# A two-layer encoder trunk: attention's DMAs in a written order, layer 0's 1/rms by TensorE, folds and transposes in the last chunk, norm weights in the splits

## The chip, the cores and the metric

The kernel runs on one core of a Trainium2 chip. Its engines are TensorE (matrix products, PE in the profile), VectorE (DVE), ScalarE (ACT), GpSimd (POOL) and SyncE (SP), which in this kernel issues nearly all DMA transfers. The metric is the device time of one execution in microseconds (us); lower is better.

## The reference

The input x has 2048 tokens of 1024 float32 values. Two layers are applied, then a final RMS norm:

```python
def rms_norm(x, g):
    y = x * lax.rsqrt(jnp.mean(x * x, axis=-1, keepdims=True) + EPS)
    return y * g

# layer 0: h = rms_norm(x, norm_even)
proj = h @ w_in                                   # 1024 -> 3072
a_x, a_b, a_c, a_z, b_u, b_z = jnp.split(proj, 6 parts of 512, axis=-1)
y_a = a_b * centred_depthwise_conv(a_c * a_x, conv_w) * silu(a_z)
f = jnp.fft.fft2(u, axes=(1, 3), norm="ortho").real     # u: b_u as (1, 2048, 4, 128)
y_b = f * silu(b_z)
x = x + jnp.concatenate([y_a, y_b], axis=-1) @ w_out

# layer 1: h = rms_norm(x, norm_odd)
q, k, v, z = jnp.split(h @ w_in, [1024, 1280, 1536], axis=-1)   # 8 q heads, 2 kv heads of 128
q = apply_rope(rms_norm(q, q_gain)); k = apply_rope(rms_norm(k, k_gain))
p = softmax(q k^T * 128 ** -0.5)                  # over all 2048 keys
x = x + ((p @ v) * silu(z)) @ w_out

return rms_norm(x, final_norm)
```

The product is computed to about float32 accuracy.

## The kernel before

**Layout and precision.** Activations are kept transposed: 128 features on the partitions, tokens along the free axis, in four token blocks of 512. Each float32 operand of a product is split into a high and a low part (`split`, lines 42 and 44: ScalarE casts the high part, VectorE or GpSimd subtracts for the low one), and each product is three matmuls (`mm3`, lines 58 to 60: high x high, high x low, low x high) into one PSUM bank. Large products take two token blocks and two halves of features and columns at once and need seven block multiplies in place of eight (class `Pairs`). The operands of the seven are named in the order in which they are multiplied: 11, s2, 12, s3, s1, 22, s4; their weights 11, t2, 21, t3, t1, t4, 22. A multiply of this kind has 24 matmuls of 512 columns. Raw weights are fetched four blocks of 512 KB at a time into a ring (`raw_weights`, line 266, with the DMA at 272) and then split (`split_weights`). A "hook" is a function run ahead of a named multiply.

**What sets the order.** TensorE's instructions run in program order through the whole kernel (`tc.manual_schedule` for PE). In stretches marked with a further `manual_schedule`, other engines do too: VectorE, ScalarE and GpSimd through the start of layer 0, VectorE and ScalarE through attention. Everywhere else a planner orders each engine's queue, SyncE's DMA issues among them, by its own cost estimates. Each engine then works its queue in that order.

**Layer 0's input projection** (`layer0_in`, to about 525 us). The first columns of u are multiplied for token blocks 0 and 1 while VectorE and ScalarE form the sums of squares in `accs`. `rstd_d` (lines 96 to 102) transposes a block's sums by TensorE, adds them, takes the power -0.5 on GpSimd and stores the result to DRAM; `bcast_d` (line 109) fetches it back, spread over all partitions. VectorE then applies norm and weight (line 427) and the operands are split. Chunks of `Pairs` products follow: the first pair of token blocks through chunks 0 to 3 and one for b_z, then the same for the second pair, 11 in all. For token blocks 2 and 3 the sums' mean and the broadcast are done by TensorE (`rstd_pe`, lines 113 to 139: eight one-column matmuls, a power, eight VectorE operations that form the identity scaled by 1/rms in two parts, and two matmuls with ones), in chunk 2's hooks ("s2" mean of 2, "s3" broadcast of 2, "s1" mean of 3, "12" broadcast of 3), and the operands of the second pair are prepared and stored in the hooks after that (`operands`, line 222). In chunk 0 the operand s1 is added in place over the raw 21, and s3 and s1 both are made ahead of the first multiply.

**The Fourier part** (525 to about 600 us). `fold` combines tokens and their mirror images of u, once per channel group; group 0's result is transposed by TensorE (line 770, into four PSUM banks), split, and multiplied by cosine and sine matrices. The folds of groups 0 and 1 stand in the program after layer 0's last chunk and are placed by the planner; the transposes of group 0 come after that chunk in TensorE's order.

**Layer 1's projection** (`layer1_in`, to about 1220 us). `raw_weights` scales each raw block in place by norm_odd on ScalarE (line 275, four passes per block), right behind the block's load; the split follows. q and k go through their norms and rotary positions (lines 1028 to 1065).

**Attention** (`Attention`, lines 1217 to 1386). There are 32 groups (16 query tiles of 128 x 2 kv heads), each with 4 heads x 4 blocks of 512 keys. The order of PE, VectorE and ScalarE is a list of steps per slot, four slots a group:

```python
SLOT = "O0 L2 E-3 G2 L3 T4 T5 S0 E-2 S1 M0 H4 E-1 S2 M1 O1 L4 S3 M2 F T6 H5 C0 T7 M3 O2 H6 N0 H7 O3 L5 E0".split()
DRAIN = "O0 L2 E-3 G2 L3 T4 T5 H4 H5 E-2 L4 O1 L5 F T6 T7 O2 E-1 H6 L6 O3 H7 W L7 W W".split()
```

S is a score product into one of four PSUM banks; M, C, N find the rows' maximum; E is the exponential on ScalarE into `praw` (line 1319), and every second E stores praw to the tile P by DMA (line 1322; the room in P comes free when T has read it). T transposes P (line 1330); H and L split it (ScalarE, VectorE); O multiplies by v. G (once per group) adds the row sums, stores their inverses `l` to DRAM (line 1370), fetches them back over all partitions as `lb` (1372), and fetches the gate z (1375). F is `finish` of the last group: ScalarE copies the output from PSUM over lb (1382), GpSimd multiplies it by the gate, and it is stored. T, H, L, O and G trail S by 26 key tiles. The next group's queries are loaded when its first S is reached. FIRST is the list of the first five slots; "X" there runs filler steps: products of z that were left for this place, counted by `nfill`. DRAIN is the list after the last group. SyncE's order is the planner's.

**The output projection and the end.** `layer1_out_start` (line 1388) fetches the first operands and weights; it stands behind the last full slot, and the W steps of DRAIN split them. `layer1_out` (line 1412) multiplies the first pair of token blocks, then the last blocks column by column (line 1498). `finish(tb)` (line 1432) applies the final norm to a finished block and stores it.

Of the kernel before, what the change touches and what calls it, by code (L numbers as in the profile page):

```python
# [15 lines left out]
F32 = mybir.dt.float32  # L16
F32R = mybir.dt.float32r
# [95 lines left out]
def rstd_pe(c, parts, tag, n):  # L113
# [11 lines left out]
    nc.gpsimd.tensor_tensor(r[:, 0:nj], m[:, 0:nj], c.mhalf[:, 0:nj], op=ALU.pow)  # L125
    rb = [c.small.tile([P, TB], F32R, tag="rb", name=f"rb_{tag}{i}") for i in "hl"]
# [15 lines left out]
WSKIP = 1  # L142
# [4 lines left out]
class Pairs:  # L147
# [118 lines left out]
    def raw_weights(self, src, raw_tiles=None, g=None):  # L266

        raw = {}
        for b in ("11", "21", "12", "22"):
# [3 lines left out]
            if g is not None:  # L273
                for i in range(4):
                    self.nc.scalar.activation(raw[b][:, i], raw[b][:, i], AF.Copy, scale=g[:, 4 * k + i:4 * k + i + 1])  # L275
        return raw

    def split_weights(self, W, op, t, name, lo_eng="dve"):
        W[op] = self.rooms.pop() if self.rooms else tuple(self.c.wp.tile([P, 4, TB // 2], F32R, tag="w", name=f"{name}_{op}{n}") for n in "hl")
        split(self.nc, t, W[op][0][:], W[op][1][:], lo_eng=lo_eng)  # L280

    def weight_ops(self, src, name, raw_tiles=None, lo_engs={}, g=None):


        raw = self.raw_weights(src, raw_tiles, g)
# [18 lines left out]
    def queue_weights(self, src, name, g):  # L304
# [3 lines left out]
        def start():  # L308
            raw.update(self.raw_weights(src, None, g))

        def step(b):
            return lambda: self.split_weights(W, b, raw[b], name)
# [7 lines left out]
    def all_weights(self, src, name, lo_engs={}, g=None):  # L320
        W, steps = self.weight_ops(src, name, lo_engs=lo_engs, g=g)
# [94 lines left out]
def layer0_in(c):  # L416
# [59 lines left out]

    def bcast(tb):
# [27 lines left out]
    bcast(0)  # L505
    ps = batch(c, wu, hrow(G[1]), "pu_1", {1: lambda: bcast(1)})
# [17 lines left out]
    W1 = []  # L524
    s2 = pair(), pair()
    d2 = lambda k: s2[k // 2][:, k % 2]

# [5 lines left out]

    def make1():
        for k in range(4):
            tt(nc.gpsimd, a21(k), a21(k), a22(k), add)
# [8 lines left out]
    def w1(*ops):  # L545
# [26 lines left out]

    bc = {}
# [1149 lines left out]
```

## Time and profile before

| | |
|---|---|
| three runs, us | 2387.48, 2389.18, 2394.09 (median 2389.18) |
| profiled execution, us | 2389.2, of which the span 2387.4 |
| TensorE busy | 2284.1 us, 96% of the span |
| VectorE | 1502.5 us, 63% |
| ScalarE | 1238.4 us, 52% |
| GpSimd | 562.1 us, 24% |

The span is the time from the first to the last instruction that the profile records. In rows of single instructions, the first number is the start in us from the span's start and the second the duration; then come engine, line of the kernel, operation, output<-inputs and shape. In rows of waits, "A <- B: total, times, longest" says that engine and instruction A stood until B had ended. SPq is SyncE's queue issuing DMAs. Rows of a stretch "from:to" list its length, the busy time and count of PE, PEld (weight loads), VectorE, ScalarE and GpSimd, and then TensorE's granted clock (1.00 is full speed), the mean busy share of the DMA engines and the GB/s moved.

### The profile page before, as it was taken

Reading aid. Unit: us, or ns where it says so; the run is one execution under the profiler, and the core shown is the slowest. Engines: PE = TensorE matmul, PEld = TensorE weight load, DVE = VectorE, ACT = ScalarE, POOL = GpSimd, SP = SyncE. Lnnn points to the kernel's source line nnn. Section 1 sums busy time; section 2 is a strip of 40 time slices with the busy share of each in tenths; the row PEclk is TensorE's granted clock in tenths of the full one; section 3 lists DMA queues with packets and bytes.
Section 4 is the critical chain, followed back from the end, with each engine's and each line's share of the span. In section 5 each row is a group of like instructions: output and inputs, shape, how many; then the busy total and the mean of one; then the engine's idle time right before and its main releaser. Section 6 shows DMA issues by size and latency. Waiting matters only on the chain. (4 is left out here: it accounts for less than half of the span.)

```text
span 2387.4 us, 34207 instructions
## 1 busy us (share of the span) xinstructions
PE 2284.1 (96%) x12438; PEld 1922.5 (81%) x12438; DVE 1502.5 (63%) x2335; ACT 1238.4 (52%) x2676; POOL 562.1 (24%) x418
## 2 busy tenths in 40 slices
PE   8889899998999989999999999999999999997998
PEld 6767788877888889889977878778788888886887
DVE  6867757679543335334437877777777777776235
ACT  5432433224333355445546777777777777775222
POOL 2455524444222122203201110000000001003212
PEclk9999999999999999999999999999999999999999
DMA  5245742166655443434465777777777777769553
GB/s 165 71 143 169 236 148 71 63 220 241 246 190 181 116 133 117 160 115 133 160 245 150 201 202 192 195 187 197 196 201 190 186 194 186 186 177 298 162 192 133
DMA packets 260568, 414.51 MB, mean 174 GB/s; under 512 B 37168, under 2 KB 157104, under 8 KB 258608
## 3 DMA queue, kind: packets, MB, share of 16 engines
q1 hardware_dynamic: 258128, 404.70, 57.3%
q0 software_dynamic: 1008, 6.55, 0.8%
q8 instruction: 99, 1.62, 0.3%
q10 hardware_dynamic: 1264, 1.07, 0.1%
q14 instruction: 69, 0.57, 0.1%
HBM read 191.45 MB, written 86.59 MB: 116 GB/s over the span
## 5 line engine op out<-in xcount | busy, mean ns | idle before, releaser
L1300 DVE TENSOR_REDUCE mx<-s 128x1 f32<-128x512 f32 x512 | 351.5, 687 | 186.9 <-PE s L60 182.7
L1319 ACT ACTIVATE praw<-s,nb,qs 128x512 f32<-128x512 f32 x512 | 400.3, 795 | 70.3 <-DMA P<-praw 52.4
L1342 ACT CAST pr<-t 128x512 fp32r<-128x512 f32 x512 | 288.2, 596 | 159.3 <-PE t L1330 159.2
L1346 DVE TENSOR_TENSOR pr<-t,pr 128x512 fp32r<-128x512 f32 x512 | 329.6, 680 | 31.4 <-ACT pr L1342 30.9
L58 PE MATMUL s<-kv,aq 128*128 128x512 f32 x512 | 215.3, 421 | 26.2 <-ACT praw L1319 22.5
L1330 PEld LDWEIGHTS t<-ident_r,P 128*128 128x128 f32 x2048 | 202.6, 140 | 40.3 <-DMA P<-praw 3.3
L58 PE MATMUL o<-pr,kv 128*128 128x512 f32 x512 | 212.9, 416 | 1.8 <-ACT pr L1342 1.7
L1330 PE MATMUL t<-ident_r,P 128*128 128x128 f32 x2048 | 204.4, 243 | 4.1 <-DMA P<-praw 3.1
L59 PE MATMUL o<-pr,kv 128*128 128x512 f32 x512 | 203.1, 397 | 0.2 <-DVE pr L1346 0.2
L60 PE MATMUL o<-pr,kv 128*128 128x512 f32 x512 | 203.2, 397 | 0.0
L60 PE MATMUL s<-kv,aq 128*128 128x512 f32 x512 | 203.2, 397 | 0.0
L59 PE MATMUL s<-kv,aq 128*128 128x512 f32 x512 | 202.1, 395 | 0.0
L275 ACT ACTIVATE ring_r<-ring_r,g1s 128x256 f32<-128x256 f32 x160 | 68.9, 498 | 188.8 <-DMA ring_r<-w 188.6
L1383 POOL TENSOR_TENSOR az<-az,lb 128x512 f32<-128x512 f32 x32 | 41.5, 1296 | 480.4 <-ACT lb L1382 480.4
L58 PEld LDWEIGHTS s<-kv,aq 128*128 128x128 f32 x512 | 96.3, 188 | 57.1 <-ACT praw L1319 37.4
L952 POOL TENSOR_TENSOR acc<-acc,sq 128x512 f32<-128x512 f32 x48 | 69.2, 1442 | 244.4 <-ACT sq L950 226.3
L60 PEld LDWEIGHTS o<-pr,kv 128*128 128x128 f32 x512 | 96.7, 189 | 23.4
L60 PEld LDWEIGHTS s<-kv,aq 128*128 128x128 f32 x512 | 96.8, 189 | 22.7
L58 PEld LDWEIGHTS o<-pr,kv 128*128 128x128 f32 x512 | 96.4, 188 | 19.2 <-ACT pr L1342 2.2
L59 PEld LDWEIGHTS o<-pr,kv 128*128 128x128 f32 x512 | 96.9, 189 | 17.8 <-DVE pr L1346 0.5
L1377 POOL TENSOR_TENSOR az<-az,lb 128x512 f32<-128x512 f32 x32 | 42.0, 1312 | 291.9 <-DMA lb<-ld 224.0
L1319 ACT ACTIVATION_READ_ACCUMULATOR praw<-s,nb,qs 128x1 f32 x512 | 110.5, 216 | 0.0
(639 smaller groups left out, 5869.6 us busy)
## 6 DMA issues: line engine op xcount, KB each, us to landing
P<-praw SPq DMA_DIRECT2D x256, 512.0 KB
ring_r<-w SPq DMA_DIRECT2D x80, 512.0 KB
ring_o<-x_T SPq DMA_DIRECT2D x32, 512.0 KB
ring_r<-wo SPq DMA_DIRECT2D x32, 512.0 KB
qT<-ring_o SPq DMA_DIRECT2D x64, 256.0 KB
aq<-qT SPq DMA_DIRECT2D x31, 512.0 KB
x1T<-po_t SPq DMA_DIRECT2D x16, 512.0 KB
a_x<-x1T SPq DMA_DIRECT2D x16, 512.0 KB
```

The lines of the kernel that those rows point to most:

```text
L58: nc.tensor.matmul(ps, lh, rh, start=first, stop=False, skip_group_check=shared)
L59: nc.tensor.matmul(ps, lh, rl, start=False, stop=False, skip_group_check=shared)
L60: nc.tensor.matmul(ps, ll, rh, start=False, stop=last, skip_group_check=shared)
L275: self.nc.scalar.activation(raw[b][:, i], raw[b][:, i], AF.Copy, scale=g[:, 4 * k + i:4 * k + i + 1])
L952: nc.gpsimd.tensor_tensor(a, a, sq, op=ALU.add)
L1300: self.nc.vector.tensor_reduce(st.mx[h][:, b:b + 1], st.banks[h, b][:], op=ALU.max, axis=AX.X)
L1319: self.exp = nc.scalar.activation(raw[:, b % 2], st.banks.pop((h, b))[:], AF.Exp, bias=st.nb[h][:], scale=self.c.qs[:, st.g[0], st.g[1], h ...
L1330: self.nc.tensor.transpose(pt[:, h * P:(h + 1) * P].bitcast(F32R), st.Ps[h // 2][:, h % 2, kt // 8, (kt % 8) * P:(kt % 8 + 1) * P], self.c ...
L1342: self.nc.scalar.copy(pr[:, 0], pt[:])
L1346: self.nc.vector.tensor_tensor(pr[:, 1], pt[:], pr[:, 0], op=ALU.subtract)
L1377: nc.gpsimd.tensor_tensor(st.zt[:], st.zt[:], st.rb[:], op=ALU.mult)
L1383: nc.gpsimd.tensor_tensor(st.zt[:], st.zt[:], st.rb[:], op=ALU.mult)
```

## The change

Layer 0: token blocks 0 and 1 get their mean and broadcast by `rstd_pe` too, as steps inside the second u batch; the inverse rms is stored to DRAM as well, for the later folds. The operand s1 has two tiles of its own, made on GpSimd ahead of chunk 0; the next chunk's weights are fetched from hook 1 on, and its weights t2, t3 are made one hook apart. In chunk 2, the broadcasts of blocks 2 and 3 stand two multiplies behind the means, and the four preparations of operands each come one hook or more later. The last chunk (number 10) gets hooks that run the folds of groups 0 and 1 and group 0's transposes, which become a function. The norm weights of layer 1 go from `raw_weights` to `split_weights`. One tile (rb_n1_1_2) is taken from another pool.

Attention: SLOT and DRAIN get the steps A (load the next group's queries), D (store the row sums' inverse), B (fetch them back, and z) and V (output stores that `finish` has queued); SyncE runs in program order through the loop. `layer1_out_start` moves three slots on, and its W steps start behind it. Seven filler steps in place of five run ahead of the first slot. The final norm of block 1 moves behind the second column of block 2.

```diff
-def rstd_pe(c, parts, tag, n):
+def rstd_pe(c, parts, tag, n, d=None):
...
     nc.gpsimd.tensor_tensor(r[:, 0:nj], m[:, 0:nj], c.mhalf[:, 0:nj], op=ALU.pow)
+    if d is not None:
+        nc.sync.dma_start(d[0:nj].rearrange("j t -> t j"), r[:, 0:nj])
...
-WSKIP = 1
...
-    def raw_weights(self, src, raw_tiles=None, g=None):
+    def raw_weights(self, src, raw_tiles=None):
...
-            if g is not None:
-                for i in range(4):
-                    self.nc.scalar.activation(raw[b][:, i], raw[b][:, i], AF.Copy, scale=g[:, 4 * k + i:4 * k + i + 1])
...
+    def split_weights(self, W, op, t, name, lo_eng="dve", g=None):
...
+        for i in range(4):
+            k = 4 * (int(op[0]) - 1) + i
+            self.nc.scalar.activation(hi[:, i], t[:, i], AF.Copy, scale=g[:, k:k + 1])
+            self.nc.vector.scalar_tensor_tensor(lo[:, i], t[:, i], g[:, k:k + 1], hi[:, i], op0=ALU.mult, op1=ALU.subtract)
...
+    def mean(tb):
+        d = None
+        if tb < 2:
+            d = c.RD0[tb] = c.dram.tile([4, P], F32, name=f"rd_n0_{tb}", tag=f"rd_n0_{tb}")
+        bc[tb] = rstd_pe(c, [accs[:, tb * TB:(tb + 1) * TB] if tb < 2 else acc1[0][:, tb - 2]], f"n0_{tb}", TB, d)
+
     def bcast(tb):
-        c.RD0[tb] = rstd_d(c, accs[:, tb * TB:(tb + 1) * TB], f"n0_{tb}")
-        RB[tb] = bcast_d(c, c.RD0[tb], f"n0_{tb}")
+        RB[tb] = c.evp.tile([P, TB], F32, tag="ev", name=f"rb_n0_{tb}")[:]
+        nc.scalar.copy(RB[tb], bc[tb]())
...
-    bcast(0)
-    ps = batch(c, wu, hrow(G[1]), "pu_1", {1: lambda: bcast(1)})
+    ps = batch(c, wu, hrow(G[1]), "pu_1", {1: lambda: mean(0), 3: lambda: (bcast(0), mean(1)), 5: lambda: bcast(1)})
...
+    s1 = [etile(f"s1_{i}") for i in range(2)]
+    d1 = lambda k: s1[k // 2][:, k % 2]
...
+    for k in range(4):
+        tt(nc.gpsimd, d1(k), a21(k), a22(k), add)
...
-        0: lambda: (make3(), make1()),
-        1: lambda: (all_k("s2", d2), make4()),
+        0: make3,
+        1: lambda: (all_k("s2", d2), make4(), first_w1()),
         2: lambda: all_k("s3", a11),
-        3: lambda: all_k("s1", a21),
-        4: first_w1,
-        5: lambda: w1("11"),
-        6: lambda: w1("t2", "t3"),
+        4: lambda: w1("11"),
+        5: lambda: w1("t2"),
+        6: lambda: (w1("t3"), all_k("s1", d1)),
         7: lambda: w1("t1"),
...
-             2: {"s2": lambda: mean1(2), "s3": lambda: bcast1(2), "s1": lambda: mean1(3),
-                 "12": lambda: (bcast1(3), st.held.clear()), "22": prepare(0)},
-             3: {"11": prepare(1), "s3": prepare(2), "12": prepare(3)}}
+             2: {"s2": lambda: mean(2), "s1": lambda: (bcast(2), mean(3)),
+                 "22": lambda: (bcast(3), st.held.clear()), "s4": prepare(0)},
+             3: {"s2": prepare(1), "s1": prepare(2), "22": prepare(3)}, 10: c.fourier_first}
...
+def fold_transposes(c, g, q):
+    nc = c.tc.nc
+    qt = c.QT[g] = c.big.tile([P, 2, 4, TB], F32R, tag="S", name=f"fqt{g}")
+    for j in range(4):
+        pt = c.ps.tile([P, TB], F32, tag="b", name=f"pt{g}_{j}")
+        for k in range(4):
+            nc.tensor.transpose(pt[:, k * P:(k + 1) * P], q[j][:, k * P:(k + 1) * P], c.ident[:])
+        split(nc, pt[:], qt[:, 0, j], qt[:, 1, j])
...
-    transposes(0, F[0][0])
...
+    SLOT = "O0 L2 E-3 G2 L3 T4 T5 S0 E-2 A S1 M0 H4 E-1 D2 B2 V S2 M1 O1 L4 S3 M2 F T6 H5 C0 T7 M3 O2 H6 N0 H7 O3 L5 E0".split()
+    DRAIN = "O0 L2 E-3 G2 L3 T4 T5 H4 H5 E-2 D2 B2 V L4 O1 L5 F T6 T7 O2 E-1 H6 L6 O3 H7 W L7 W W".split()
...
+            if kind == "V":
+                run_all(self.ended)
+                continue
+            if kind == "A":
+                if n % 4 == 1 and n // 4 + 1 < len(self.groups):
+                    self.group(n // 4 + 1)
+                continue
...
-        d = c.dram.tile([4, P], F32, name=f"ld{nm}", tag=f"ld{nm}")
-        nc.sync.dma_start(d[:].rearrange("h t -> t h"), l[:])
+
+    def D(self, k):
+        if k % NTT:
+            return
...
+        self.nc.sync.dma_start(st.d[:].rearrange("h t -> t h"), st.l[:])
+
+    def B(self, k):
+        if k % NTT != 8:
+            return
...
-        nc.sync.dma_start(
+        self.ended.append(lambda: nc.sync.dma_start(
...
-    finish(1)
...
         a2, _ = columns(2, slice(0, TB), m)
+        if m == 1:
+            finish(1)
...
-                c.fold0, c.fold1 = fold(c, 0), fold(c, 1)
+                c.fourier_first = {"s2": fold0, "12": fold1, "22": lambda: fold_transposes(c, 0, c.fold0[0])}
...
-        for _ in range(5):
+        for _ in range(7):
             next(fill)
-        att = Attention(c, qp, *pools, groups, fill, [6, 6, 6, 6, 3])
+        att = Attention(c, qp, *pools, groups, fill, [6, 6, 6, 5, 2])
...
-            for i in range(5, n):
-                att.slot(i, att.WARM if c.late and i > 5 else att.SLOT)
-            att.pieces = layer1_out_start(c, lp)
-            for i in range(n, n + att.LATE // 4 + 2):
-                att.slot(i, att.DRAIN if i > n + WSKIP else [s for s in att.DRAIN if s != "W"])
+            with tc.manual_schedule(engines={mybir.EngineType.SP}):
+                for i in range(5, n):
+                    att.slot(i, att.WARM if c.late and i > 5 else att.SLOT)
+                for i in range(n, n + att.LATE // 4 + 2):
+                    if i == n + 3:
+                        att.pieces = layer1_out_start(c, lp)
+                    att.slot(i, att.DRAIN if i > n + 3 else [s for s in att.DRAIN if s != "W"])
+                att.flush()
+                run_all(att.ended)
             att.split_all()
-            att.flush()
```

More of the change, by code (lines that the diff above doesn't have):

```diff
@@ L318, in queue_weights, with all_weights @@
         return W
-    def all_weights(self, src, name, lo_engs={}, g=None):
-        W, steps = self.weight_ops(src, name, lo_engs=lo_engs, g=g)
+    def all_weights(self, src, name, lo_engs={}):
+        W, steps = self.weight_ops(src, name, lo_engs=lo_engs)
         for f in steps.values():
@@ L475, in layer0_in @@
     c.RD0 = {}
+    bc = {}
+    c.ones = c.small.tile([P, P], F32R, name="ones0", tag="sq", bufs=1)
+    nc.scalar.activation(c.ones[:], c.ident[:], AF.Copy, bias=1.0, scale=0.0)
+    def mean(tb):
[3 more added lines that the diff above has]
+        bc[tb] = rstd_pe(c, [accs[:, tb * TB:(tb + 1) * TB] if tb < 2 else acc1[0][:, tb - 2]], f"n0_{tb}", TB, d)
     def bcast(tb):
-        c.RD0[tb] = rstd_d(c, accs[:, tb * TB:(tb + 1) * TB], f"n0_{tb}")
-        RB[tb] = bcast_d(c, c.RD0[tb], f"n0_{tb}")
+        RB[tb] = c.evp.tile([P, TB], F32, tag="ev", name=f"rb_n0_{tb}")[:]
+        nc.scalar.copy(RB[tb], bc[tb]())
     def u_out(tb, ps):
@@ L571, in stats1 @@
                     square(x[:, i], k + i, acc1[0][:, tb - 2], x[:, i], nc.vector if tb == 3 else nc.gpsimd)
-    bc = {}
-    c.ones = c.small.tile([P, P], F32R, name="ones0", tag="sq", bufs=1)
-    nc.scalar.activation(c.ones[:], c.ident[:], AF.Copy, bias=1.0, scale=0.0)
-    def mean1(tb):
-        bc[tb] = rstd_pe(c, [acc1[0][:, tb - 2]], f"n0_{tb}", TB)
-    def bcast1(tb):
-        RB[tb] = c.evp.tile([P, TB], F32, tag="ev", name=f"rb_n0_{tb}")[:]
-        nc.scalar.copy(RB[tb], bc[tb]())
     def conv_chunk(pr, ch, W, hooks={}):
@@ L658, in out @@
                 nc.sync.dma_start(dst[m + i, :, j * TB:(j + 1) * TB], t[:, i])
-        st.product(W, out, f"p{name}_")
+        st.product(W, out, f"p{name}_", hooks)
     def next_weights(i):
@@ L682, in layer0_in @@
         elif ch == 4:
-            simple_chunk(pr, W, c.bz, True, f"z{pr}")
+            simple_chunk(pr, W, c.bz, True, f"z{pr}", hooks.get(i, {}))
         else:
@@ L760, in fourier @@
     nc.sync.dma_start(dcos, c.dcos_d)
-    QT = [None] * 4
+    QT = c.QT
     NY = [None] * 4
@@ L768, in nyquist @@
         nc.vector.tensor_tensor(nyq[:, 1:2], nyq[:, 0:1], nyq[:, 2:3], op=ALU.add)
-    def transposes(g, q):
-        qt = QT[g] = c.big.tile([P, 2, 4, TB], F32R, tag="S", name=f"fqt{g}")
-        for j in range(4):
-            pt = c.ps.tile([P, TB], F32, tag="b", name=f"pt{g}_{j}")
-            for k in range(4):
-                nc.tensor.transpose(pt[:, k * P:(k + 1) * P], q[j][:, k * P:(k + 1) * P], c.ident[:])
-            split(nc, pt[:], qt[:, 0, j], qt[:, 1, j])
     def second(g, z, f, par):
@@ L849, in fourier @@
         if g < 3:
-            transposes(g + 1, F[g + 1][0])
+            fold_transposes(c, g + 1, F[g + 1][0])
         second(g, z, f, 0)
@@ L1232, in __init__ @@
         self.done = set()
-        self.last = None
+        self.last, self.ended = None, []
     def slot(self, n, names):
@@ L1588, in trunk_kernel, with fold0, fold1 @@
                 c.pairs = Pairs(c)
+                c.QT = [None] * 4
+                def fold0():
+                    c.rb01 = c.pairs.gtile("rb01")[:, 0:D]
+                    for tb in range(2):
+                        bcast_d(c, c.RD0[tb], f"u_{tb}", tile=c.rb01[:, tb * TB:(tb + 1) * TB])
+                    c.fold0 = fold(c, 0)
+                def fold1():
+                    c.fold1 = fold(c, 1)
+                c.fourier_first = {"s2": fold0, "12": fold1, "22": lambda: fold_transposes(c, 0, c.fold0[0])}
                 layer0_in(c)
                 c.pairs.renew()
-                c.rb01 = c.pairs.gtile("rb01")[:, 0:D]
-                for tb in range(2):
-                    bcast_d(c, c.RD0[tb], f"u_{tb}", tile=c.rb01[:, tb * TB:(tb + 1) * TB])
-                c.fold0, c.fold1 = fold(c, 0), fold(c, 1)
                 fourier(c)
```

35 lines of the change are left out of this document (18 added, 17 removed).

## The prediction

> **What bounds the kernel now.** I read the page first (busy time by engine), then what TensorE waited for over the whole span, then the same list stage by stage, and last the instructions in order of time around each wait.
>
> ```profile
> span 2387.4 us, 34207 instructions
> PE 2284.1 (96%) x12438; PEld 1922.5 (81%) x12438; DVE 1502.5 (63%) x2335; ACT 1238.4 (52%) x2676; POOL 562.1 (24%) x418
> ```
>
> TensorE is busy 2284.1 of 2387.4 us and no other engine passes 63%. The change leaves TensorE nearly all its work, so what it can win lies in the 103.3 us in which TensorE stands, and in what a stand costs afterwards. Who makes it stand:
>
> ```profile
> PE s L58 <- ACT praw L1319: 22.5, 32, 2.8
> PE pb_n L135 <- DVE rb_n_2h L129: 9.9, 1, 9.9
> PE po L58 <- ACT lb L1382: 7.0, 1, 7.0
> PE ptk L1046 <- POOL pk_t L1065: 7.0, 1, 7.0
> ...
> PE s L58 <- issue: 3.7, 1, 3.7
> PE pfz L58 <- ACT fqt L42: 3.4, 1, 3.4
> PE t L1330 <- DMA P<-praw: 3.1, 1, 3.1
> ```
>
> Columns: total us, times, longest. The edits touch the place of each of these rows, so I price them place by place. One more price is needed everywhere: what follows a long stand.
>
> ```profile
> 2184.95 0.39 PE L59 MATMUL po<-a_o,wo_11h 128*128 128x512 f32 x1
> 2185.18 0.40 PE L60 MATMUL po<-a_o,wo_11l 128*128 128x512 f32 x1
> ...
> 2193.16 0.63 PE L59 MATMUL po<-a_o,wo_11h 128*128 128x512 f32 x1
> 2193.59 0.63 PE L60 MATMUL po<-a_o,wo_11l 128*128 128x512 f32 x1
> ```
>
> Ahead of the 7.0 us stand one 512-column matmul starts 0.23 us after another; behind it, 0.43. The slow pace lasts some eight matmuls, so about 1.6 us is lost on top. A multiply of 24 such matmuls at 0.23 takes 5.5 us; this is my unit of distance below.
>
> **The change part by part.**
>
> **(1) Layer 0's first two token blocks.** Now:
>
> ```profile
> 36.73 0.36 SPq L102 DMA_DIRECT2D rd_n<-r_n  x1
> 46.54 0.33 SPq L109 DMA_DIRECT2D rb_n<-rd_n  x1
> 59.50 0.33 SPq L109 DMA_DIRECT2D rb_n<-rd_n  x1
> ```
> ```profile
> 51.57 2.74 DVE L427 SCALAR_TENSOR_TENSOR x<-x,g0s,rb_n 128x512 f32<-128x512 f32 x4 [12.64 <-DMA rb_n<-rd_n]
> ```
> ```profile
> 98.53 1.62 SPq L272 DMA_DIRECT2D ring_r<-w  x3
> ```
> ```profile
> PE pa_s L60 <- DVE w_t2l L44: 1.7, 1, 1.7
> PE pa L58 <- ACT w_11h L42: 1.5, 1, 1.5
> PE pa L58 <- ACT wa_11h L42: 1.5, 1, 1.5
> PE pa L60 <- DVE w_11l L44: 1.5, 1, 1.5
> PE pa_s L58 <- ACT w_t2h L42: 1.3, 1, 1.3
> PE pa L60 <- DVE wa_11l L44: 1.2, 1, 1.2
> ```
>
> Block 0's 1/rms leaves at 36.7 and is back for VectorE at 51.6; VectorE stands 12.64 us. Block 1's is fetched only at 59.5. VectorE then runs late up to 104, which gives the waits on wa_11 (2.7 us together) and, because the next chunk's weights are fetched only at 98.5, when the first operand "s1" frees its room, the waits on w_11 and w_t2 (6.0). In the new order the mean of block 0 stands two contraction steps into the second batch (2 x 12 x 0.23 = 5.5 us), its broadcast 5.5 us later. The chain that stands for block 3 below (a VectorE operation, a power on GpSimd, eight VectorE operations) takes about 5 us when nothing is queued ahead, so the broadcast meets finished data. But ScalarE's order now has block 1's broadcast copy (after step 5, near 48.5) ahead of the casts of "11", and VectorE has eight more operations ahead of the norms: I get the casts 3 to 4 us earlier than the 52.4 implied by the row at 51.57, not 8. That covers the 2.7. With "s1" in rooms of its own the weight loads go out about one multiply or more earlier, which covers the 6.0. Added on TensorE: eight one-column matmuls and four broadcasts against eight transposes, under 1 us. Sum -8; bounds -10 (all gone) and -3 (only half gone).
>
> **(2) Blocks 2 and 3.** The broadcast moves from one to two multiplies behind the mean.
>
> ```profile
> 160.85 0.95 PE L122 MATMUL pm_n<-inv_d,ring_o 128*128 128x1 f32 x8
> ```
> ```profile
> 172.89 0.15 DVE L123 TENSOR_SCALAR m_n<-pm_n 128x4 f32<-128x4 f32 x1
> ...
> 177.23 1.14 DVE L130 SCALAR_TENSOR_TENSOR rb_n_2l<-ident,r_n,rb_n_2h 128x128 fp32r<-128x128 f32 x4
> ```
>
> The chain takes 17.5 us (160.85 to 178.4), 12 of them because the first VectorE operation sits behind older work. Two multiplies and the mean give 12 us. If that queue stays, 5.5 of the 9.9 us go; if it shrinks, all 9.9 plus block 3's smaller waits and two slow stretches, some 16 at most. I take -8, nearer the first since nothing shortens the queue. The other side: the four preparations of the second pair's operands each come one multiply later, and their stores and loads have to end before that pair's first chunk. Bounds -1 and +5 (one multiply), value +1.
>
> **(3) First folds and transposes in layer 0's last chunk.**
>
> ```profile
> 520.63 1.07 ACT L655 ACTIVATE pz_p<-pz 128x512 f32<-128x512 f32 x2
> ```
> ```profile
> 525.19 1.91 PE L775 MATMUL pt<-ident,uo 128*128 128x128 f32 x16
> ```
>
> The folds already run beside that chunk. New is that the transposes stand one multiply earlier, so their splits run under the last multiply, and the 3.4 us wait goes, with some 1.6 us of slow pace. Against it: the transposes need four PSUM banks, two of which the activation at 520.6 frees, and they would stand at about 519.4. A wait of 2 us is likely there. Value -3; bounds -6 and +3.
>
> **(4) Norm weights in the splits.**
>
> ```profile
> 842.75 1.71 ACT L275 ACTIVATE ring_r<-ring_r,g1s 128x256 f32<-128x256 f32 x4 [4.92 <-DMA ring_r<-w]
> ```
>
> Today ScalarE scales each block as it lands: here it stood 4.92 us for a load, and the squares of k's RoPE, for which the transposes wait 7.0 us, are queued behind it. In the new form the scaling is the cast, one ScalarE pass of this duration per block in place of two, at the time of the split, when the load is long in; VectorE gets four 256-column operations for one. Both engines have room under the matmuls. If the wait on loads was the cause, those 7.0 and 1.6 of slow pace go; if the planner only puts something else there, nothing, or 2 us more. Value -3; bounds -9 and +2.
>
> **(5) Attention.**
>
> ```profile
> SPq L1372 <- DMA ld<-l: 181.7, 21, 10.1
> ...
> SPq L1322 <- PE t L1330: 65.2, 26, 2.8
> ```
> ```profile
> 1560.31 0.36 SPq L1370 DMA_DIRECT2D ld<-l  x1
> ...
> 1572.37 0.34 SPq L1372 DMA_DIRECT2D lb<-ld  x1
> ```
> ```profile
> 1577.55 0.78 ACT L1319 ACTIVATE praw<-s,nb,qs 128x512 f32<-128x512 f32 x1 [2.84 <-DMA P<-praw]
> ```
>
> Once per group SyncE issues the load of the row sums' broadcast right behind their store and stands up to 10.1 us for it; the stores of P behind it go out late, ScalarE finds no free praw, and S waits. The new list puts the load two slots (some 14 us) behind the store, the query load, the output store and the rest each into a slot of its own, so at issue all are ready. That removes the cause of the 22.5 us. The two fill steps moved ahead of the first S (6 x 0.23 = 1.4 us) come off the 3.7. Value -22, bounds -26 and -10 (P late for bandwidth in half the groups).
>
> **(6) The drain and the start of the output projection.**
>
> ```profile
> 2166.35 0.78 SPq L1370 DMA_DIRECT2D ld<-l  x1
> ...
> 2183.52 0.33 SPq L1372 DMA_DIRECT2D lb<-ld  x1
> ```
> ```profile
> 2160.00:2220.00 60.00, 50.02 (x235) 40.02 (x236) 33.17 (x37) 32.28 (x47) 20.65 (x15) 0.91 0.99 286
> ```
>
> The P store that makes T wait 3.1 us is late for the same block as in (5); it goes, with 1.6 of slow pace. The projection's loads (4 MB) now start three slots later, behind the last row sums' store, which now takes 17 us to its load under them. But the last broadcast load is queued behind those 4 MB; at the 286 GB/s of this stretch (its last column; the DMA engines, the column before, are busy 0.99) that is 14 us, so I expect the last output copy still some 5 us late in place of 7.0, and the splits of the first operand to be just in time. Value -6; bounds -15 (both stands and their slow pace gone) and +4 (operand late).
>
> **(7) The second block's final norm, two columns later.** It takes one stall away:
>
> ```profile
> PE po L60 <- DVE wo_22l L44: 1.4, 1, 1.4
> ```
>
> and puts its eight VectorE operations nearer the tail, where VectorE works for the last blocks. Value -1, bounds -2 and +4.
>
> **The sum.** -8 -8 +1 -3 -3 -22 -6 -1 = -50. The profiled execution took 2389.2 us, 1.8 more than its span; the median of the three runs is 2389.18, so nothing has to be shifted: 2339 us. All bounds at their good ends: -85, 2304; all at their bad ends: 0, 2389.
>
> **The rivals.** *The waits of layer 0 and the projections only move* (parts 1 to 4 give nothing): the planner orders VectorE, ScalarE and GpSimd outside the hand-ordered stretches, and each removed wait uncovers the next queue. For it speaks the 12 us queue in (2); against it, that (1) lies in a hand-ordered stretch. -29: 2360.
>
> *Bandwidth, not the block, makes P late*: then (5) gives nothing. For it, in a stretch of that stage:
>
> ```profile
> 1560.00:1620.00 60.00, 57.66 (x332) 47.46 (x331) 45.78 (x87) 43.17 (x101) 5.13 (x4) 1.00 0.74 185
> ```
>
> the DMA engines are busy 0.74 of the time. Against it: 0.74 isn't full, 185 GB/s is far from the 286 above, and SyncE's row in (5) names the store it waits for. -28: 2361.
>
> *Everything goes*: (1), (2), (5) and (6) near their good ends, -75: 2314.
>
> *SyncE's fixed order becomes the wait.* In program order nothing overtakes. A group's first P store already waits up to 2.8 us for a room that TensorE frees; now the query load and the second P store stand behind it. Parts outside (5) bring -28. Attention has 32 groups and loses 22.5/32 = 0.7 us in each; from 0.7 + 28/32 = 1.6 us in each on, the whole is slower. At 2.2 it is 32 x 1.5 = +48, and -28: 2409. The Trainium skill, "DMA: Bandwidth & Descriptors", section "Anatomy of one DMA", speaks for this rival: the DMA engines don't wait on semaphores, the issuing sequencer does, ahead of dispatch, so one waiting transfer holds all behind it. The rows of (5) agree (10.1 us). Against: every transfer but that first P is ready long before its turn.
>
> *The order is the same in effect* (the late weights and the 10 us store come back elsewhere): 2389.
>
> For the slow pace, the Trainium skill, "TensorE: Matmul & The Clock Gate", Part 1, says the clock halves after an idle window of about 3.4 us. The pace of 0.43 behind the 7.0 us stand agrees. By it the waits of (5) carry no second loss, as I have summed; had each of the 32 cost 1.6 us more, (5) would be -73.
>
> **How the numbers follow.** Forecast 0.50, layer 0 moves 0.18, everything goes 0.12, fixed order waits 0.08, bandwidth 0.07, no effect 0.05. Faster: 0.50 + 0.18 + 0.12 + 0.07 = 0.87; slower 0.08; within 0.3% (7 us, about what a measurement tells from no change) 0.05. The likeliest case alone spans 2322 to 2356. The range takes in layer 0 moving and bandwidth, and all of "everything goes" but its edge: 2310 to 2372; the slower case, no effect and the edges are left out.
>
> **What would show it.** In the profile after: the rows of SyncE on ld and of S on praw gone or under 5 us; the pb_n wait near 5 us; no 12.64 us stand of VectorE; the w_11 and w_t2 waits gone; the fqt wait gone and perhaps a new one before pt; a wait on lb near 5 us at the projection's start. The forecast is wrong if S still waits over 10 us in all, if new waits before 1200 us sum to over 15, or if the projection's first operand is late.

## The result

The changed kernel took 2336.72 us in the median of four runs (2335.16 to 2337.82), the kernel before 2390.75 on the same chip: a ratio of 0.9773, 95% interval 0.9757 to 0.979. The prediction was 2339. The sum came out 2 us from the measured time; its terms did not, and a second chip, further down, gave another ratio.

The page of the changed kernel, and then the rows of what TensorE waited for, over the whole span (total us, times, longest):

```profile
span 2334.1 us, 34356 instructions
PE 2265.6 (97%) x12450; PEld 1917.2 (82%) x12450; DVE 1531.9 (66%) x2469; ACT 1201.3 (51%) x2638; POOL 571.1 (24%) x418
```
```profile
PE po L58 <- ACT lb L1408: 9.9, 1, 9.9
PE pa_s L58 <- DVE pa_u L395: 6.0, 2, 5.7
...
PE pfz L59 <- DMA fm<-fmat: 4.7, 2, 2.7
PE pz L60 <- DVE w_21l L44: 4.7, 1, 4.7
PE pfz L58 <- DMA fm<-fmat: 3.3, 1, 3.3
PE pfz L58 <- DMA fme<-feven: 2.5, 2, 1.4
...
PE s L58 <- ACT praw L1333: 1.2, 2, 0.9
```

S waits 1.2 us where it waited 22.5; the waits on the broadcast of block 2, on k's and q's transposes, on w_11 and on fqt's cast are gone. New are a stand of 5.7 us for a PSUM bank that VectorE frees (pa_u), 4.7 for a weight split (w_21), 10.5 for the tables of the Fourier part (fm, fme), and the stand on lb has grown from 7.0 to 9.9.

Where the time went, by the starts and ends of the first and last matmul of some tiles in TensorE's timelines (us; the last column is what the stage gained):

| until | before | after | ahead by | gained in the stage |
|---|---|---|---|---|
| first pa_s (chunk 1) | 112.0 | 103.8 | 8.2 | 8.2 |
| first pz (end of chunk 3) | 246.9 | 230.7 | 16.2 | 8.0 |
| last pz_s (end of the last chunk) | 525.4 | 514.1 | 11.3 | -4.9 |
| first po (end of the Fourier start) | 593.2 | 585.7 | 7.5 | -3.8 |
| first fill (end of layer 1's projection) | 1220.0 | 1200.0 | 20.0 | 12.5 |
| last S | 2149.2 | 2093.4 | 55.8 | 35.8 |
| last O | 2184.9 | 2124.9 | 60.0 | 4.2 |
| last po | 2376.2 | 2323.0 | 53.2 | -6.8 |

From the third group to the 31st, a group of attention takes 27.96 us in place of 28.86; a further 9 us are won between the first fill step and the third group. There the 3.67 us stand ahead of the first S has become one of 1.21, and the dozen matmuls behind it that started 0.43 us apart now start 0.23 apart. In the steady part (1290 to 2090 us) TensorE is now busy in all of the 800 us, before in 782.

SyncE's queue over the steady part (1290 to 2090 us) and in one group shows the new order. What it waits for now is ScalarE's next praw, which is its pace, and no longer its own store:

```profile
SPq L1336 <- ACT praw L1333: 383.7, 143, 4.7
SPq L1336 <- ACT pr L1356: 131.7, 82, 1.9
SPq L1336 <- PE t L1344: 93.0, 29, 3.3
```
```profile
1581.70 0.54 SPq L1389 DMA_DIRECT2D ld<-l  x1
1586.11 2.47 SPq L1336 DMA_DIRECT2D P<-praw  x2
1588.68 2.18 SPq L1410 DMA_DIRECT2D oT<-az  x1
1593.09 2.48 SPq L1336 DMA_DIRECT2D P<-praw  x2
1595.66 0.76 SPq L1398 DMA_DIRECT2D lb<-ld  x1
```

The fetch of lb leaves 13.96 us behind its store, with four P stores in between.

### The profile page after: what moved, and what is told of

It is laid out like the page before. It is cut to its first block, busy times and chain, and to the rows that moved or that the text cites. A ratio compares the mean times of both kernels' runs of the same rounds, so it can differ in the third digit from the quotient of the medians.

```text
span 2334.1 us, 34356 instructions
## 1 busy us (share of the span) xinstructions
PE 2265.6 (97%) x12450; PEld 1917.2 (82%) x12450; DVE 1531.9 (66%) x2469; ACT 1201.3 (51%) x2638; POOL 571.1 (24%) x418
## 5 line engine op out<-in xcount | busy, mean ns | idle before, releaser
L58 PE MATMUL s<-kv,aq 128*128 128x512 f32 x512 | 211.0, 412 | 2.4 <-DMA aq<-qT 1.2
L60 PE MATMUL s<-kv,aq 128*128 128x512 f32 x512 | 201.9, 394 | 0.0
L59 PE MATMUL s<-kv,aq 128*128 128x512 f32 x512 | 200.8, 392 | 0.0
L60 PEld LDWEIGHTS s<-kv,aq 128*128 128x128 f32 x512 | 96.1, 188 | 22.5
L58 PEld LDWEIGHTS s<-kv,aq 128*128 128x128 f32 x512 | 95.8, 187 | 21.3 <-ACT praw L1333 3.2
L59 PEld LDWEIGHTS s<-kv,aq 128*128 128x128 f32 x512 | 96.3, 188 | 17.2
```

The lines of the kernel that those rows point to most:

```text
L58: nc.tensor.matmul(ps, lh, rh, start=first, stop=False, skip_group_check=shared)
L59: nc.tensor.matmul(ps, lh, rl, start=False, stop=False, skip_group_check=shared)
L60: nc.tensor.matmul(ps, ll, rh, start=False, stop=last, skip_group_check=shared)
```

## The experiments

The runs were made on two chips. On one, where bank, lb_early, fold_back and norm_raw ran, the kernel before took 2388.26 us; on the other, where all others ran, 2357.09 and 2357.75. The changed kernel took 2331.02 there. So runs are compared within a chip. Which chip gave the result above is not on record; its times agree with those of the first, and it is counted with them. The diffs show the main lines of an edit, with "..." for what is left out.

### The same two kernels on the second chip

> The kernel before, unchanged, profiled beside the changed one on one chip. On one chip it took 2388 us, on another 2357, while kernels with the new attention took 2334 to 2337 on both. Theory: what differs between chips is the time that S waits for praw (22.5 us in the first profile) and no other stage; where this run takes about 2357 us, the row of S on praw is under 8 us and SyncE's row on ld under 100 us. Rival (another stage, or the clock): the row of S stays near 20 us and the difference lies elsewhere. If it takes about 2389 us, the rows are those of the first profile, and what the other chip does differently stays open.

> The changed kernel, unchanged, on the chip of the run above. Theory: its time doesn't depend on the chip, 2334 to 2338 us, S waits under 2 us in all. Rival: it moves with the kernel before, near 2305 us where that takes 2357.

Measured: 2360.63 us for the kernel before (the seven runs beside it: median 2357.75) and 2331.02 for the changed one (2329.62 to 2331.99): ratio 0.99, interval 0.9875 to 0.9925. The gain is 27 us there and 54 on the first chip. The changed kernel differs by 6 us between the chips, a little more than the expectation allowed, the one before by 33.

TensorE's and SyncE's waits of the kernel before, in the steady part, on the second chip:

```profile
PE s L58 <- ACT praw L1319: 1.5, 3, 0.7
```
```profile
SPq L1372 <- DMA ld<-l: 205.1, 26, 10.0
```

and SyncE's row of the first profile for the same stretch:

```profile
SPq L1372 <- DMA ld<-l: 192.2, 22, 10.5
```

The row of S is under 8 us, as the theory said. The row on ld is not under 100: SyncE stands there for its store as it did on the first chip, but 205.1 / 26 = 7.9 us at a time in place of 192.2 / 22 = 8.7. From the issue of the store to that of the fetch it is 9.14 us against 10.04, in the mean of 28 groups of each SyncE timeline. A group takes 28.06 us there and 28.86 on the first, and of the 28.6 us between the two spans 27.6 lie between the first fill step and the last S; the other stages differ by up to 3 us each way and nearly cancel. The stand behind the store was just hidden on one chip and just not on the other. That the later fetch makes the difference is read from these rows; no run changed it alone. Why the store lands earlier on one chip isn't shown by these runs.

### Attention alone

The kernel before with the class Attention and the loop of the changed one. Short form of the edit:

```diff
-    SLOT = "O0 L2 E-3 G2 L3 T4 T5 S0 E-2 S1 M0 ...
+    SLOT = "O0 L2 E-3 G2 L3 T4 T5 S0 E-2 A S1 M0 H4 E-1 D2 B2 V S2 ...
+            with tc.manual_schedule(engines={mybir.EngineType.SP}):
```

> The kernel before with the attention part alone (the lists with A, D, B, V, SyncE in program order, filler steps, the later start of the output projection). Theory (parts add up): the attention stages of the changed kernel gained 9.0 us at their start and 26.1 in the steady part and nothing at the drain, so 2390.8 - 35 = 2356 us, 27.97 us a group. Rival (part of that came from the earlier stages): 2362 to 2368 us, and the loads ahead of the first slot late.

Measured: 2350.65 us (8 runs) beside 2357.09 on the second chip, 6.4 less, ratio 0.9967 (0.9954 to 0.9979). A group takes 27.96 us as in the changed kernel, so the part does by itself what it does there; but on this chip there were only 28.06 - 27.96 = 0.1 us a group to win. The expectation took the first chip's 2390.8 for granted; the 35 us it asked for were not there to be had, and no run shows attention alone on the first chip.

### Order or distance

```diff
-    SLOT = "... G2 L3 T4 T5 S0 E-2 A S1 M0 H4 E-1 D2 B2 V S2 ...
+    SLOT = "... G2 D2 B2 L3 T4 T5 S0 E-2 A S1 M0 H4 E-1 V S2 ...
-        if k % NTT != 8:
+        if k % NTT:
```

> The changed kernel with one edit: SyncE stays in program order, but the row sums' store, their fetch as lb and the gate's fetch are issued in the slot of G, one behind the other, as in the kernel before. Theory (the distance between store and fetch): SyncE stands for its own store once a group, P stores go out late and S waits again, 0.7 us a group or more: 2358 to 2365 us. Rival (the planner's order was what made P late, the program order cures it): 2337 to 2341 us, with S waiting under 3 us in all.

```diff
-            with tc.manual_schedule(engines={mybir.EngineType.SP}):
-                for i in range(5, n):
+            for i in range(5, n):
```

> The changed kernel with one edit: SyncE's order through attention is left to the planner, with the steps A, D, B, V where they are. Theory (distance): the planner may put a fetch behind its store again, but the steps are two slots apart in the program, so most of the gain stays: 2338 to 2348 us. Rival (the order): S waits 15 to 25 us again, 2358 to 2365 us.

With program order but no distance: 2485.54 us, 154 us above the changed kernel. With distance but the planner's order: 2334.73, 3.7 above it, which the spread of the runs (2331.93 to 2338.59 against 2329.62 to 2331.99) does not separate. Waits of the first over the whole span, the steady part (length, busy TensorE, weight loads, VectorE, ScalarE, GpSimd, granted clock, DMA share, GB/s), and two stands with the S matmuls that follow:

```profile
PE s L58 <- ACT praw L1333: 97.9, 32, 5.9
```
```profile
1290.00:2090.00 800.00, 721.81 (x3862) 590.95 (x3862) 548.80 (x1026) 506.77 (x1180) 64.45 (x59) 0.93 0.49 167
```
```profile
1599.74 0.79 PE L58 MATMUL s<-kv,aq 128*128 128x512 f32 x1 [2.96 <-ACT praw L1333]
1600.33 0.63 PE L59 MATMUL s<-kv,aq 128*128 128x512 f32 x1
...
1632.35 0.50 PE L58 MATMUL s<-kv,aq 128*128 128x512 f32 x1 [3.02 <-ACT praw L1333]
...
1634.16 0.63 PE L58 MATMUL s<-kv,aq 128*128 128x512 f32 x1
1634.59 0.63 PE L59 MATMUL s<-kv,aq 128*128 128x512 f32 x1
```

This is the prediction's rival of the fixed order, made real: S waits 3.1 us a group, and a group takes 33.12 us, 5.16 more than 27.96. The other 2 us a group go with the slow pace: behind 26 of the 29 stands between 1290 and 2260 us matmuls take 0.63 us and start 0.43 apart, at once (the first stand shown) or 1.3 to 1.9 us later (the second), for 4 to 11 matmuls of 512 columns; the granted clock of the stretch is 0.93. I had expected the wait of the kernel before, 0.7 us a group. What I had left out is that the planner had not put store and fetch back to back: a P store went out between them. SyncE's queue of sp_planner shows the same:

```profile
1583.25 0.37 SPq L1389 DMA_DIRECT2D ld<-l  x1
1583.71 0.47 SPq L1336 DMA_DIRECT2D P<-praw  x1
1591.85 0.34 SPq L1398 DMA_DIRECT2D lb<-ld  x1
```

The planner ignored the distance of the steps and issued the fetch as the kernel before does, 9.04 us behind the store in the mean; a group takes 28.19 us, as in the kernel before on this chip. So this run does not test the distance without the order: the planner took the distance away. What the runs show is that the list without the order leaves the steady part as it was on this chip, and that the order without the distance is the worst of all.

### Norm weights

```diff
+            if g is not None:
+                for i in range(4):
+                    self.nc.scalar.activation(raw[b][:, i], raw[b][:, i], AF.Copy, scale=g[:, 4 * k + i:4 * k + i + 1])
```

> The changed kernel with part (4) undone: norm_odd's weights applied to the raw blocks right behind their loads. Theory: the scalings that wait for their load in ScalarE's queue hold up k's and q's norms, so the 7.0 and 3.0 us waits of the transposes come back: 2347 to 2350 us. Rival (the planner's order had put them there by chance, and other parts moved it): no wait over 3 us, 2334 to 2340 us.

Measured: 2352.06 us, 14.9 above the 2337.16 of the run named bank on that chip, which is the changed kernel in effect (below); the theory asked for 10 to 13. The waits are back, within 0.3 us of what they were, and so is ScalarE's stand for a load ahead of the squares of k:

```profile
PE ptk L1055 <- POOL pk_t L1074: 7.3, 1, 7.3
...
PE ptq L1055 <- POOL rs_q L1037: 3.2, 1, 3.2
```
```profile
837.21 1.71 ACT L276 ACTIVATE ring_r<-ring_r,g1s 128x256 f32<-128x256 f32 x4 [5.80 <-DMA ring_r<-w]
838.83 0.35 ACT L1030 ACTIVATE sq_k<-pk,rs 128x128 f32<-128x128 f32 x1
```

### Folds and transposes

```diff
-             3: {...}, 10: c.fourier_first}
+             3: {...}}
...
+    fold_transposes(c, 0, F[0][0])
...
+                fold0()
+                fold1()
```

> The changed kernel with part (3) undone: folds and group 0's transposes behind layer 0's last chunk, as before. Theory: with the transposes early, their split tile takes the room that the tables fme and fm had, and the tables' loads leave GpSimd at 508 us in place of 498, so the Fourier part waits 10 us for them; undone, these waits go and the 3.4 us wait on the split with its slow pace comes back: 2331 to 2335 us. Rival (the prediction's part 3, worth 3 us the other way): 2339 to 2341 us.

Measured: 2328.84 us, 8.3 below the run named bank, more than the theory's 2 to 6. The issues of the tables' loads by GpSimd, in the kernel before and then in the changed one:

```profile
498.07 1.13 POOL L753 DMA_DIRECT2D fme<-feven  x2 [1.12 <-PE pz_s L60]
505.12 1.10 POOL L758 DMA_DIRECT2D fm<-fmat  x2
...
516.00 1.11 POOL L758 DMA_DIRECT2D fm<-fmat  x2
```
```profile
508.11 1.14 POOL L768 DMA_DIRECT2D fme<-feven  x2
509.23 2.13 POOL L773 DMA_DIRECT2D fm<-fmat  x4
```

In the changed kernel fqt takes its tile from the pool ahead of fme and fm, and GpSimd issues fme behind both folds, 10 us later. The waits on fm and fme (4.7 + 3.3 + 2.5) are gone in this run and the two on fqt are back (7.3 and 3.3). 4.1 us of the gain lie in the Fourier part, by the start of the first po in both timelines (583.1 against 587.2); another 3.2 appear only in the output projection, where the planner ordered the splits otherwise (the wait on wo_22 is 2.0 in the one and under 1 in the other); what moved them isn't shown. Whether it is the room or GpSimd's queue that makes the tables late wasn't told apart.

### Blocks 2 and 3, and the room of s1

```diff
+             2: {"s2": lambda: mean(2), "s3": lambda: bcast(2), "s1": lambda: mean(3),
+                 "12": lambda: (bcast(3), st.held.clear()), "22": prepare(0)},
+             3: {"11": prepare(1), "s3": prepare(2), "12": prepare(3)}, 10: c.fourier_first}
```

> The changed kernel with part (2) undone: the broadcasts of blocks 2 and 3 one multiply behind their means and the operands prepared one hook earlier, as before. In the changed kernel the 9.9 us wait for the broadcast is gone, but TensorE stands 5.7 us for a PSUM bank that VectorE frees late, and 4.7 us for a weight split in the first b_z chunk, which were not there. Theory (the two multiplies of distance are worth their prediction): the broadcast waits come back and the others shrink: 2341 to 2346 us. Rival (VectorE's queue is what is late, and the wait only changes its place): 2334 to 2339 us.

Measured: 2336.86 us, 5.8 above the changed kernel's 2331.02 on that chip. The numbers expected stood on the first chip's 2336.7; by differences, the theory asked for 4 to 9 us, the rival for -3 to +2. The broadcast's wait is back at 10.1 us, and the two new stands of the changed kernel are not there. So part (2) takes away a wait of 10.1 and is worth about half of it. Where the other half went, the changed kernel's rows show, TensorE's and then VectorE's:

```profile
148.63 0.94 PE L122 MATMUL pm_n<-inv_d,ring_o 128*128 128x1 f32 x8
...
162.17 0.80 PE L58 MATMUL pa_s<-as,w_t1h 128*128 128x512 f32 x1 [5.72 <-DVE pa_u L395]
...
169.15 0.39 PE L137 MATMUL pb_n<-rb_n_2h,ones 128*128 128x512 f32 x1
```
```profile
161.44 1.27 DVE L395 TENSOR_TENSOR pa_u<-pa_p,pa_s 128x512 f32<-128x512 f32 x2
162.63 0.15 DVE L123 TENSOR_SCALAR m_n<-pm_n 128x4 f32<-128x4 f32 x1
```

The stand on pa_u lies between block 2's mean and its broadcast, and the VectorE operation that ends it stands right ahead of the first one on the mean (m_n). VectorE's queue is as late as before: m_n comes 14.0 us behind the mean, where it came 12.0 behind it in the kernel before. TensorE now waits for that queue at pa_u, 5.7 us and some ten matmuls at the slow pace, instead of 9.9 at the broadcast. The 4.7 us stand on w_21 has a counterpart with the old hooks: there the waits on w_t1l and on pz_w are 4.0 and 2.5 where they are 1.6 and 1.6 in the changed kernel on this chip.

```diff
+            tt(nc.gpsimd, a21(k), a21(k), a22(k), add)
...
+        0: lambda: (make3(), make1()),
+        1: lambda: (all_k("s2", d2), make4()),
...
+        3: lambda: all_k("s1", a21),
+        4: first_w1,
+        5: lambda: w1("11"),
+        6: lambda: w1("t2", "t3"),
```

> The changed kernel with half of part (1) undone: s1 added in place over the raw 21 with its split ahead of the first weights' loads, the loads in hook 4, t2 and t3 in one hook; TensorE's broadcast of the first two blocks stays. Theory: the waits on w_11 and w_t2 (6.0 us in the kernel before) come back and those on wa_11 stay away: 2340 to 2343 us. Rival (the earlier broadcast alone moved the loads up enough): 2336 to 2338 us.

Measured: 2333.61 us, 2.6 above the changed kernel; by differences the theory asked for 3 to 6 and the rival for -1 to +1. TensorE's waits from 90 to 240 us:

```profile
PE pa_s L60 <- DVE w_t2l L44: 1.7, 1, 1.7
PE pa_s L58 <- ACT w_t2h L42: 1.5, 1, 1.5
PE pa L60 <- DVE w_11l L44: 1.5, 1, 1.5
PE pa L58 <- ACT w_11h L42: 1.2, 1, 1.2
```

The four waits (5.9 us) are back and those on wa_11 are not, as the theory said; but the stand on pa_u, 4.6 us in the changed kernel on this chip, is gone. TensorE then comes to the mean of block 2 at 158.6 us in place of 149.4 and doesn't stand on pa_u or at the broadcast; in the changed kernel it comes earlier and waits. So VectorE takes about half of what the earlier weights give, and the stand on pa_u goes when either part is undone.

### The stand ahead of the output projection

```diff
+    c.kept = [c.ps.tile([P, TB], F32, tag="b", name=f"kept{i}") for i in range(2)]
+        if fresh and name.startswith("po") and name.endswith("22") and getattr(self.c, "kept", None):
+            ps, self.c.kept = self.c.kept, None
...
+                att.split_all()
                 att.flush()
```

> The changed kernel with two edits at the start of the output projection: the first multiplies take other PSUM banks (the two first tiles are kept for the block that is begun last), and the splits of operand 12 stand ahead of the last output copy in ScalarE's order. In the changed kernel TensorE stands 9.9 us there, until ScalarE's copy to lb. Theory (the bank): the second tile of the projection lies in the bank that still holds the last group's output, so the stand is gone although lb comes no earlier; operand 12 costs 0 to 3 us in its place: 2323 to 2328 us. Rival (a late operand behind SyncE's queue; the copy only happens to end then): TensorE still stands 8 to 10 us, on a split: 2335 to 2338 us.

Measured: 2337.16 us, with the stand at 9.6. That looks like the rival, but the experiment did not make what it meant to: in the built program the first two tiles of the projection still lay in banks 0 and 7, and 7 is the bank of the last attention output (the trace doesn't name banks); and the last output copy still stood ahead of operand 12's casts in ScalarE's order. It is the changed kernel again.

```diff
+    fetch()
     c.wo1_raw = st.raw_weights(c.wo1[0])
...
+                        att.pieces = layer1_out_start(c, lp, lambda: att.B(last))
```

> The changed kernel with one edit: the last group's fetch of lb and z goes between the first operand's loads and the weights' loads of the output projection, not behind the 4 MB. In the changed kernel that fetch leaves SyncE at 2123.7 us and GpSimd stands for its z until 2132.9. Theory: the copy then runs right behind the last O, so the 9.9 us stand falls to 1 to 2 us, and the weights and operands come 1 to 2 us later: 2327 to 2331 us. Rival (ScalarE's casts of later operands hold the copy, wherever lb is): 2335 to 2338 us.

Measured: 2333.98 us, 3.2 below the run named bank with two runs of each, less than the theory asked for. The stand on lb is gone, so the copy was late mainly for lb and z. ScalarE's casts held it for the rest: in the changed kernel GpSimd's multiply with z ends at 2134.2 us, and the copy starts at 2136.4, behind two casts. But the 4 MB come later and the weights take its place, with the slow pace behind it:

```profile
2127.72 0.80 PE L58 MATMUL po<-a_o,wo_11h 128*128 128x512 f32 x1 [1.15 <-ACT wo_11h L42]
...
2132.68 0.80 PE L60 MATMUL po<-a_o,wo_11l 128*128 128x512 f32 x1 [3.74 <-POOL wo_11l L44]
```

The last run goes to the cause, and takes the folds back as well:

```diff
-                 for n, b in (("pss", 4), ("pst", 3), ("pso", 1))]
+                 for n, b in (("pss", 4), ("pso", 1), ("pst", 3))}
...
             if kind == "F":
-                self.flush()
+                if n < 4 * len(self.groups) + 6:
+                    self.flush()
...
+                att.split_all()
                 att.flush()
                 run_all(att.ended)
-            att.split_all()
```

> The changed kernel with three edits: folds and transposes behind the last chunk again; the bank of the attention output placed between the four S banks and the three T banks, so that the projection's tile that shares it is begun with the fifth multiply in place of the first; and the last group's output copy behind the W steps in ScalarE's order. (In the run named bank the first two tiles had stayed in banks 0 and 7, and 7 is the bank of the last output, so that its edit had moved nothing, and the copy stood ahead of the W steps.) Theory (the bank holds TensorE): the 9.9 us stand goes with its slow pace, operand 12 costs 0 to 4 us in its place; with the 8 us of the folds' return 2318 to 2324 us. Rival (late operands hold TensorE just as long): 2327 to 2330 us.

Measured: 2318.77 us (2316.6 to 2321.26) beside 2331.02 for the changed kernel and 2357.75 for the one before, ratio 0.9851 to the latter (0.9824 to 0.9877). TensorE's longest waits from 2090 us on, then some of the first matmuls of the projection in the changed kernel and in this one, with the last output copy of this one:

```profile
PE po L60 <- POOL wo_11l L44: 1.7, 1, 1.7
PE pb_n L137 <- DVE rb_n_1h L131: 1.6, 1, 1.6
PE po L60 <- DVE wo_21l L44: 1.5, 1, 1.5
```
```profile
2126.65 0.50 PE L60 MATMUL po<-a_o,wo_11l 128*128 128x512 f32 x1 [1.33 <-POOL wo_11l L44]
2137.04 0.80 PE L58 MATMUL po<-a_o,wo_11h 128*128 128x512 f32 x1 [9.89 <-ACT lb L1408]
2137.63 0.63 PE L59 MATMUL po<-a_o,wo_11h 128*128 128x512 f32 x1
```
```profile
2120.61 0.50 PE L60 MATMUL po<-a_o,wo_11l 128*128 128x512 f32 x1 [1.75 <-POOL wo_11l L44]
2120.95 0.39 PE L58 MATMUL po<-a_o,wo_11h 128*128 128x512 f32 x1
2121.18 0.39 PE L59 MATMUL po<-a_o,wo_11h 128*128 128x512 f32 x1
```
```profile
2133.21 0.58 ACT L1410 COPY lb<-o 128x512 f32<-128x512 f32 x1
```

The fourth matmul is the first of the second tile, the one in bank 7, and it reads the same operands as the first matmul. With the bank moved, its stand and the 0.43 us pace behind it are gone, and nothing of more than 1.7 us takes their place. The copy ends 12.8 us after that matmul starts, and TensorE doesn't wait for it. The bank held TensorE, not an operand. Between this run and the changed kernel's second profile, 5.0 us are won by the last O, with the folds back, and 9.3 from there to the last po.

## Why the prediction was right in sum and wrong in its terms

- **The reading of the whole** held: TensorE bounds the kernel, its work hardly changed (2284.1 to 2265.6 us busy), and 53 us came out of its stands and what follows them.
- **(1), -8**: 8.2 at its place. The sum is right there, but it left out the cost downstream: s1's half wins 5.9 us at its place and 2.6 in the end, because TensorE then comes too early for VectorE's queue. What the earlier broadcast is worth in the end, no run shows by itself.
- **(2), -8 and +1**: the stage gained 8.0, and the run with the old hooks gives what the part is worth: 5.8 us. That is close to the 5.5 that the working gave for a queue that stays, and it did stay. The value of 8 less 1 was too high, and what I had wrong is where the rest of the wait would stand: not at the broadcast, whose row is gone, but at pa_u, ahead of it.
- **(3), -3**: the term that had the wrong sign. The working named the PSUM banks as the risk (0.5 us in the profile after) and left out that the fold's tile and GpSimd's folds come ahead of the tables' loads. The part costs 8.3 us, 4.1 of them at its place, outside its bounds of -6 and +3 either way. The 4.9 us that the table shows lost up to the last pz_s are not taken apart by any run.
- **(4), -3**: the mechanism was right, the choice of value wrong. Of the two cases named, the wait on loads was the cause, for q's 3.0 us too, and the part is worth 14.9 us (bound -9). The working had priced k's 7.0 with its slow pace and not q's. (The squares queued there are those of k's norm, not of its RoPE.)
- **(5), -22**: on the first chip 35.8 from the first fill step to the last S, on the second, by the same rows, 8.3. The mechanism holds: the praw waits go when the fetch leaves long enough behind its store, 13.96 us where I had 14. The size was that of one chip: the 22.5 us were what was left of a stand of 8.7 us that other work almost covered, and with 0.9 us less from store to fetch only 1.5 are left in the steady part. Of the 9 us won ahead of the third group I had counted 1.4; the slow pace behind the 3.7 us stand was not in the sum. And "right behind their store" was not how the planner had it: a P store went out in between.
- **(6), -6**: +2.6 (4.2 won in the drain, 6.8 lost at the start of the projection). I had "the last output copy still some 5 us late"; TensorE stood 9.9 for it, and I had not asked what the copy holds: a PSUM bank that the second tile needs. The slow pace behind it lasted 13 matmuls, not eight.
- **(7), -1**: no run shows it by itself. The stall that it was to take away, 1.4 us on wo_22, is still there: 2.5 in the profile after, 1.3 on the second chip.
- **The signs of being wrong**: one of the three came. The new waits before 1200 us, pa_u, w_21 and the tables, sum to 20.9 us, and the line was drawn at 15. S waits 1.2 and not over 10, and the projection's first operand costs 1.3. The wait on lb was to be near 5 and is 9.9.
- **The rivals**: "the waits only move" is half true of (1) to (3), and false of (4). The bandwidth rival is out: DMA engines carry 198 GB/s in the steady part on the second chip after the change and S doesn't wait. The fixed order as the wait is real, at 33.12 us a group, where store and fetch stand together; with two slots between them it costs nothing.

By the stages of the table, (4) and (5) gave 23 us more than predicted, (1) and (2) 1 more, (3) 12 less, (6) and (7) 10 less; the 3 us by which the profile's gain of 53.2 passes 50 are what was left. That these errors cancel is luck. On the second chip the gain was 27 us, about half the forecast. There, the runs that undo or isolate a part give 6.4 for attention, 5.8 for (2) and 2.6 for half of (1), and on the first chip 14.9 for (4) and -8.3 for (3): together 21 of the 27. The rest is open.

The prediction quoted the Trainium skill, "TensorE: Matmul & The Clock Gate", Part 1, for an idle window of about 3.4 us. The trace agrees only roughly. In the run with store and fetch together, 25 of the 29 stands were between 2.6 and 3.2 us, shorter than that window, and 22 of these brought the slow pace. The stands of the kernel before in its steady part, 1.8 us at most, brought none, but those of 1.72 us at 114.5 and of 1.87 us at 195.6 did, and so did the longest wait on praw, 2.8 us at 1279.6. So the sum's zero for the slow pace in (5) was not quite right either. The same section of the Trainium skill has the window run freely; that the pace drops at once in one group and 1.3 to 1.9 us later in another agrees with it. The Trainium skill's "DMA: Bandwidth & Descriptors", section "Anatomy of one DMA", says that the issuing sequencer does the waiting, in a section on transfers that GpSimd issues. SyncE's queue agrees in the run with store and fetch together, at 154 us.

## What to carry to other kernels

A queue in program order needs every transfer ready at its turn: move a fetch of what was just stored several issues behind the store, and fix the order too, since a planner may undo the distance. What a stand costs that is almost hidden can turn on less than a microsecond, so a gain read from one chip's trace isn't that of another. Where a wait is gone, look for its queue: it may hold TensorE at an earlier place, as VectorE's did between mean and broadcast. Before a wait is put down to a late operand, look which PSUM bank the next tile takes and who still reads it; and when a step moves earlier, ask whose tile and whose place in a queue it takes.

## What was not expected of the hardware

The same program differs by 33 us (1.4%) between two chips, almost all of it in attention, where one DMA round trip takes 9.14 us on one and 10.04 on the other. And a stand of about 3 us costs some 2 us more in pace, sometimes only after several matmuls at full pace: 32 of them, 97.9 us in all, made the kernel 154 us slower.
